# First block's down product with activations stationary, and the mixer's x kept by tokens

## The chip, the cores and the metric

One core of a Trainium2 chip runs the program. The metric is the time of one execution on the device in microseconds. Of the kernel before there are three timed runs, 919.45, 919.45 and 920.10, median 919.45, and one profiled execution. PE is the matrix engine (TensorE), DVE the vector engine (VectorE), ACT the scalar engine (ScalarE), POOL and SP the engines GpSimd and SyncE, which here mostly issue transfers (DMA). SBUF is the memory on the chip that the engines read, PSUM the eight accumulation banks that PE writes, each 128 partitions by 512 numbers here.

## The reference

One layer, 512 tokens, width 1024, all in 32-bit numbers:

```python
x = x + 0.5 * swiglu(rmsnorm(x, g1), w_gate1, w_up1, w_down1)   # first block, inner width 2816
x = x + token_mixer(rmsnorm(x, gm), w_in, w_out, ...)           # 4 differential + 8 dilated heads
x = x + 0.5 * swiglu(rmsnorm(x, g2), w_gate2, w_up2, w_down2)   # second block
return rmsnorm(x, g_final)

def swiglu(x, w_gate, w_up, w_down):
    return (jax.nn.silu(x @ w_gate) * (x @ w_up)) @ w_down

def rmsnorm(x, g):
    return x * lax.rsqrt(jnp.mean(x * x, axis=-1, keepdims=True) + 1e-6) * g
```

The mixer projects the normed x to q, k and v, takes scores with a bias by distance, exponentials, weighted values, a norm per differential head, and the product with w_out. lambda, a number from four small vectors, weighs the second map of the differential heads.

## The kernel before

**Numbers in two parts.** Each operand of a product is split into a high part (a cast to PE's rounded 32-bit type, on ACT) and a low part (the difference, on DVE). A product is three matmuls, high x high, high x low, low x high (`mm3`, L143 to L146). So every weight that arrives needs a cast on ACT and a subtraction on DVE before PE can use it. "High" and "low" below mean these two.

**Layout.** x lies by features in the first block (`x[k]`: 128 features by 512 tokens), as do its normed parts `xh[k]`, `xl[k]`.

**The two blocks (`ffn`, L225 to L1131).** A first part makes some pairs of inner columns plainly. The rest goes through `pipeline` (L835): a list of units, each with seven products of 2 x 2 blocks instead of eight (`SEVEN`, L46): a11, s3, s2, a12, s1, a22, s4, where s1 = a21 + a22, s2 = s1 + a11, s3 = a11 + a21 and s4 = s2 + a12 or alike. "g" and "u" units make pairs of gate and up columns. Their 4 x 3 matmuls per product take a weight block as the stationary operand and 256 tokens of x as the moving one.

The down product is where the two blocks differ. In the first block, six inner tiles go plainly ("p" units, weights stationary, 512 tokens moving, 18 matmuls for each of eight output tiles), and two groups of eight inner tiles go through "d" units: weights stationary, 256 columns of activation moving, four units in each group, each updating two output tiles of x (`down_step`, L815). In the second block the down product is turned: "P" units and "t" units take the activations as stationary and 512 columns of weight as moving operand (`tiles_product`, `block_product`, L583 to L658), so that their output, and x, lie by tokens. A "t" unit runs each of the seven products over four or five pairs, one pair a step, six matmuls of 512 columns a step.

**Sums of weight blocks.** s1 and s3 are made by transfers: SP loads one block of 256 KB into a slot, and POOL then issues a second transfer that adds the other block onto it (`weight_sums`, L364, for pair units; `block_load`, L471, for "t" units). s2 and s4 are made by DVE (`total`, L396).

**Order.** `pipeline` gives every piece of work a time in nominal nanoseconds, with `STEP` = 1410 as one product of one pair, and a rank. Pieces are issued by time, then by rank. A product stands at its own start; its high part 4 steps before (rank 3), its low part 3 steps before (rank 2.5), a total 5 steps before (rank 2), loads 7 to 14 steps before (`block_events`, L885, for "t" units). Within an engine the issued order is the order of execution; between engines, semaphores hold an instruction until its data is there and its buffer is free. In the mixer the lists `at` and `put` (L1301) do the same by the number of the chunk. At the end of the first block the order of DVE and ACT is left to a scheduler for the lines between the two (L1268 to L1282, lambda).

**Slots.** 44 slots of 128 x 512 numbers (`slot`, L99) serve one use after another. `PAIR_SLOTS` (L49) gives the seven tiles of a pair's activations their slots, the first of each seven holding the block b11, which a11 alone reads. Weight tiles from DRAM go through three buffers "raw", their two parts through `w_all`.

**Between block and mixer.** As the last "d" units finish an output tile, `to_mixer` (L1256) multiplies x with the mixer's gain, splits it into xh and xl, and adds its squares to `sq`. The mixer's norm is not applied to x: `rstd` (L195) makes it by eight 1-column matmuls (`st_n`) and spreads it by two more (`bc_n`), and q and k are multiplied with it when they leave PSUM (`scaled`, L1424), v when it is copied. q and k of a head pair take 8 chunks (`qk_chunks`, L1399), and attention 0 starts its scores four chunks after q0 and k0 are done (L1714). While the mixer runs, x is turned by DVE in 32 x 32 blocks, written to DRAM and read back by tokens (`turn_x`, `rows_back`, L1721 to L1732).

**Between mixer and second block.** `wo_tail` (L1888) adds the output product to x by tokens and norms each token tile: sum (DVE), squares with their total (ACT), mean (DVE), root (ACT), reciprocal (DVE), scaling (ACT). PE then turns the scaled tile to features by transposes (`turn`, L955).

Of the kernel before, what the change touches and what calls it, by code (L numbers as in the profile page):

```python
# [42 lines left out]
PAIRED = (6, 2)  # L43
PLAIN = 6
# [9 lines left out]
TURNED_PLAIN = 4  # L54
TURNED_PAIRS = ((4, 6, 8, 10), (12, 14, 16, 18, 20))
TURNED_SETS = {4: (28, 29, 30, 31, 32, 33, 34), 6: (35, 36, 37, 38, 39, 40, 41), 8: (42, 43, 12, 13, 14, 15, 4),
# [3 lines left out]
TURNED_FIRST = (26, 27)  # L60
TURNED_S3 = ((20, 21, 26, 27), (20, 21, 26, 27, "xh0"))
TURNED_S1 = ((8, 9, 11, 10), (10, 11, 9, 8, "xh2"))
TURNED_A22 = (("sq", "bc", "ob", 8), ("xh3", "xl3", "xh5", "xl5", "xh7"))
TURNED_AHEAD = {"s3": ((36, 32, 28, 24), (80, 77, 74, 71, 11)),
                "s1": ((19, 16, 13, 10), (19, 17, 15, 12, 9)),
                "a11": ((11, 10, 9, 8), (11, 10, 9, 8, 4))}
# [5 lines left out]
STEP, PLAIN_STEP, TILES_STEP = 1410, 4080, 5440  # L72
# [12 lines left out]
def tile_macaron(ctx: ExitStack, tc, xs, xT, wf, wgu1, wst1, wd1, wdg1, wqk, wvw, wv, wo, wgu2, wst2,  # L85
# [11 lines left out]
    dp = ctx.enter_context(tc.tile_pool(name="dp", bufs=1, space=DRAM))  # L97

# [126 lines left out]
    def ffn(wgu, wst, wd, wdg, n0, n1, norm, early, res, nm, hooks, ended, first=None,  # L225
            bias=None, final=None, lead=None):
# [98 lines left out]
        plain = 5  # L325
        if final is None:
            units = [("g", n1)] + pairs(n1 + 2, PLAIN + 8)
            units += [("p", m) for m in range(plain)] + [("d", 0, m) for m in range(0, KD, 2)]
            units += pairs(PLAIN + 8, JF)
            units += [("p", m) for m in range(plain, KD)] + [("d", 1, m) for m in range(0, KD, 2)]  # L330
        else:
            units = [("g", n1)] + pairs(n1 + 2, TURNED_PAIRS[0][-1] + 2) + [("P", 0), ("t", 0)]
            units += pairs(TURNED_PAIRS[1][0], JF) + [("P", 1), ("t", 1)]
        ops, begin, starts = [], {}, [0]
        for u in units:
            begin[u] = len(ops)
            for o in ((u[0],),) if u[0] in "pP" else SEVEN:
                for p in range({"t": len(TURNED_PAIRS[u[1] % 2]), "P": 2}.get(u[0], 1)):
                    ops.append((u, o, p))
                    starts.append(starts[-1] + {"p": PLAIN_STEP, "P": TILES_STEP}.get(u[0], STEP))  # L340

        def rows(u):

            if u[0] == "d":
                return wdg[u[1], u[2]], wdg[u[1], u[2] + 1]
            return [wst[u[1] + i - n1][int(u[0] == "u")] for i in range(2)]

        def sum_slots(u):
            if u[0] == "d":
                return GROUP_SUMS[u[2] // 2 % 2]  # L350
            if final is not None:
                if u == units[0]:
                    return TURNED_FIRST
                return GROUP_SUMS[(u[0] == "u") ^ (u[1] in TURNED_PAIRS[1])]
            if u == units[0]:
                return PAIR_SLOTS[0][:2]
            if u[1] == PLAIN + 8:
                return GROUP_SUMS[u[0] == "u"]
# [16 lines left out]
        def load(u, which=(0, 1)):  # L375
            raws.setdefault(u, [])
            whole = [wd[u[1]]] if u[0] == "p" else [rows(u)[0], rows(u)[1][:, 512:]]
# [5 lines left out]
        def source(t):  # L383
# [6 lines left out]
            if o[0] == "p":  # L390
                return r0[:, :PLAIN * P]
# [20 lines left out]
        def high(t):  # L412
            u, o, p = ops[t]
            if o[0] == "p":
                half.clear()
                h, l = w_place()
                made[t] = h[:, :PLAIN * P], l[:, :PLAIN * P]
            elif o[0] == "P":
# [4 lines left out]
            elif (u, o[0]) == (("t", 1), "s4"):  # L423
                made[t] = kept_weights(p)
            else:
# [10 lines left out]
                if not half:  # L436
                    h, l = w_place(odd)
                    half.extend([(h[:, :512], l[:, :512]), (h[:, 512:], l[:, 512:])])
                    if skip or t and ops[t - 1][1][0] == "p":

                        half.pop(0)
# [24 lines left out]
        def block_rows(u, p):  # L466
            r = wdg[TURNED_PAIRS[u[1]][p] // 2]
# [3 lines left out]
        def block_load(u, o, p):  # L471
# [7 lines left out]
            elif o == "a12":  # L479
                dst = parts["B", u, p] = place(TURNED_S3[u[1]][p], f"rb{nm}{u[1]}{p}")  # L480
                nc.sync.dma_start(dst, r["a12"])
            elif o == "a22":
                dst = parts["E", u, p] = place(TURNED_A22[u[1]][p], f"re{nm}{u[1]}{p}")
                nc.sync.dma_start(dst, r["a22"])
            else:
                k, tags, a, b = (("B", TURNED_S3, "a11", "a21") if o == "s3"
                                 else ("C", TURNED_S1, "a21", "a22"))
# [15 lines left out]
        def moving(u, block):  # L503

            if u[0] == "d":
                return [hs[PLAIN + 8 * u[1] + 2 * p][block] for p in range(4)]
# [33 lines left out]
        def product(t):  # L540
# [8 lines left out]
            if o[0] == "p":  # L549
                m = u[1]  # L550
                po = mm_bank(f"pd{nm}{m}")
                for k in range(PLAIN):
                    c = slice(k * P, (k + 1) * P)
                    mm3(po[:], h[:, c], l[:, c], ah[k][:], al[k][:], k == 0, k == PLAIN - 1)
                put(starts[t + 1], stt, x[m], po[:], 0.5, x[m], ALU.add)
                return
# [78 lines left out]
        def block_step(t, u, o, pw, pz, pv):  # L635
# [21 lines left out]
            if u[1] == 1:  # L657
                final(o, t, put, pz)  # L658
# [1416 lines left out]
```

## Time and profile before

| what | us |
|---|---|
| median of three runs (919.45 to 920.10) | 919.45 |
| the profiled execution, its own time | 920.74 |
| its span, from first to last instruction | 919.0 |
| PE busy in the span | 910.7 |
| DVE busy | 731.8 |
| ACT busy | 549.6 |
| POOL busy | 118.2 |

The first block's pair units run from about 84 to 294 us in the trace, its "p" and "d" units from 154 to 214 and from 290 to 346, the mixer from 346 to about 580, the second block from there to the end. How to read the rows: a row of a group gives the source line, the engine, the operation, output and inputs by the program's names, shape, count, and after the bars the busy time, the mean duration of one in ns, and the idle time of the engine ahead of it with what ended it. A matmul's row lasts longer than the spacing to the next one, since matmuls overlap in the array: 0.39 us for 512 columns, while the next may start 0.23 us later. What PE spends is therefore read from start to start. A timeline row gives start, duration, engine, line and operation.

### The profile page before, as it was taken

The page shows a single profiled execution, that of the slowest core. Times are in us where ns is not written, and L with a number is a line of the kernel's source. Part 1 is how long each engine was busy: PE and PEld are TensorE (multiplying, and loading weights), DVE is VectorE, ACT ScalarE, POOL GpSimd, SP SyncE. Part 2 cuts the span into 40 slices and gives each one's busy share as a digit, 9 for nine tenths or more (in the row PEclk, how much of TensorE's full clock was granted, in tenths as well). Part 3 has the DMA queues.
Part 4 walks back from the last instruction along what each step waited for, and adds up shares of the span by engine and source line. Part 5 has one row for each costly group of instructions (what it writes and reads, how often), then busy time and mean ns, then how long its engine had stood idle before and what let it go on. Part 6 is the DMA issues. An engine that isn't in the chain of part 4 may idle for free.

```text
span 919.0 us, 16498 instructions
## 1 busy us (share of the span) xinstructions
PE 910.7 (99%) x6014; PEld 830.8 (90%) x6014; DVE 731.8 (80%) x1525; ACT 549.6 (60%) x1155; POOL 118.2 (13%) x157
## 2 busy tenths in 40 slices
PE   9999999999999999999999999999999999999997
PEld 7888999899999998888989778989999889999885
DVE  7797888676888897968876545897887878888786
ACT  6455665345665665655776675656666446666564
POOL 0001100112111010063000000011121012211100
PEclk9999999999999999999999999999999999999999
DMA  7446645578856563457433204365798269877722
GB/s 256 125 142 159 163 120 162 154 173 206 218 139 178 147 169 109 144 154 236 132 115 116 69 24 138 92 158 168 179 232 216 82 181 242 210 180 204 199 70 92
DMA packets 64593, 143.66 MB, mean 156 GB/s; under 512 B 7872, under 2 KB 8384, under 8 KB 64512
## 3 DMA queue, kind: packets, MB, share of 16 engines
q1 hardware_dynamic: 47856, 110.93, 37.1%
q0 software_dynamic: 16656, 31.68, 20.2%
q8 instruction: 47, 0.77, 0.3%
q14 instruction: 34, 0.28, 0.1%
HBM read 135.20 MB, written 4.24 MB: 152 GB/s over the span
## 4 chain that ended last, share of the span: by engine, by line
PE 94%; DVE 3%; DMA 1%; ACT 1%; issue 1%; DVEq 0%; SPq 0%; ACTq 0%
PE pt L146 3%; PE pt L145 3%; PE pt L144 3%; PE pwo L144 2%; PE pwo L145 2%; PE pwo L146 2%; PE pua L144 2%; PE pua L145 2%; PE pua L146 2%; PE pq L144 2%; PE pq L146 1%; PE pq L145 1%; PE pk L144 1%; PE pk L146 1%; PE pk L145 1%; PE pda L146 1%
## 5 line engine op out<-in xcount | busy, mean ns | idle before, releaser
L1520 ACT ACTIVATE pr<-pr,mx 128x128 f32<-128x128 f32 (+3 forms) x64 | 36.0, 563 | 37.7 <-DVE mx L1517 37.6
L1517 DVE CUSTOM_DVE_ANT_0 pr<-sc,strip 128x128 f32<-128x128 f32 (+3 forms) x64 | 30.6, 487 | 19.6 <-PE sc L1515 19.4
L372 POOL DMA_DIRECT2D s1bg<-wst_dram x10 | 8.7, 866 | 272.9 <-DVE fin L1908 160.8
L443 ACT CAST w<-s2a 128x512 fp32r<-128x512 f32 x46 | 28.6, 621 | 16.1 <-DVE s2a L406 13.2
L447 DVE TENSOR_TENSOR w<-s2a,w 128x512 fp32r<-128x512 f32 x46 | 31.5, 686 | 6.6 <-ACT w L443 6.6
L447 DVE TENSOR_TENSOR w<-s2b,w 128x512 fp32r<-128x512 f32 x38 | 26.1, 686 | 6.8 <-ACT w L443 6.8
L1726 POOL DMA_DIRECT2D xn_rows<-xt x32 | 20.6, 654 | 64.1 <-DVE xt L1723 64.1
L443 ACT CAST w<-s2b 128x512 fp32r<-128x512 f32 x38 | 23.5, 620 | 5.7 <-DVE s2b L406 5.4
L144 PE MATMUL pq<-xh,w 128*128 128x512 f32 x64 | 26.7, 417 | 0.0
L144 PE MATMUL pwo<-w,mh 128*128 128x512 f32 x64 | 25.9, 404 | 0.0
L146 PE MATMUL pq<-xh,w 128*128 128x512 f32 x64 | 25.1, 392 | 0.0
L145 PE MATMUL pq<-xl,w 128*128 128x512 f32 x64 | 25.1, 392 | 0.0
L144 PE MATMUL pk<-xh,w 128*128 128x512 f32 x64 | 25.1, 391 | 0.0
L146 PE MATMUL pk<-xh,w 128*128 128x512 f32 x64 | 25.0, 391 | 0.0
L145 PE MATMUL pwo<-w,mh 128*128 128x512 f32 x64 | 25.0, 391 | 0.0
L146 PE MATMUL pwo<-w,ml 128*128 128x512 f32 x64 | 25.0, 391 | 0.0
L145 PE MATMUL pk<-xl,w 128*128 128x512 f32 x64 | 24.9, 390 | 0.0
L1324 DVE TENSOR_TENSOR w<-raw_qk,w 128x512 fp32r<-128x512 f32 x28 | 19.0, 687 | 4.6 <-ACT w L1320 4.5
L146 PE MATMUL pwgb<-xh,w 128*128 128x256 f32 x80 | 22.6, 282 | 0.0
L145 PE MATMUL pxgb<-ttb,w 128*128 128x256 f32 x80 | 22.5, 281 | 0.0
L145 PE MATMUL pwgb<-xl,w 128*128 128x256 f32 x80 | 22.5, 281 | 0.0
L144 PE MATMUL pwgb<-xh,w 128*128 128x256 f32 x80 | 22.5, 281 | 0.0
(712 smaller groups left out, 3945.7 us busy)
## 6 DMA issues: line engine op xcount, KB each, us to landing
raw_qk<-wqk_dram SPq DMA_DIRECT2D x16, 512.0 KB, 3.4
raw0bg<-wst_dram SPq DMA_DIRECT2D x10, 512.0 KB, 5.3
raw0bu<-wst_dram SPq DMA_DIRECT2D x9, 512.0 KB, 5.4
raw_gua<-wgu_dram SPq DMA_DIRECT2D x8, 512.0 KB, 3.3
raw0ag<-wst_dram SPq DMA_DIRECT2D x8, 512.0 KB, 4.8
raw0ad<-wdg_dram SPq DMA_DIRECT2D x8, 512.0 KB, 3.8
strip<-bias_rows SPq DMA_DIRECT2D x16, 256.0 KB, 3.8
raw_wo<-wo_dram SPq DMA_DIRECT2D x8, 512.0 KB, 3.4
```

Of the source, the lines that this page charges most:

```text
L144: T.matmul(po, wh, mh, start=first, stop=False, skip_group_check=on)
L145: T.matmul(po, wh, ml, start=False, stop=False, skip_group_check=on)
L146: T.matmul(po, wl, mh, start=False, stop=last, skip_group_check=on)
L372: nc.gpsimd.dma_start(t[:], b, accum_op=ALU.add)
L443: A.copy(made[t][0], source(t))
L447: V.tensor_tensor(l, source(t), h.bitcast(F32), op=ALU.subtract)
L1324: V.tensor_tensor(l[:, c:c + 512], raw[:, c:c + 512], h[:, c:c + 512].bitcast(F32), op=ALU.subtract)
L1517: V.tensor_tensor_reduce(out=pi, in0=ps[:, :w], in1=st["b"][m][:, w - 1::-1], op0=ALU.add, op1=ALU.min, scale=1.0, scalar=3.0e38, accum_ou ...
L1520: A.activation(pi, pi, AF.Exp, scale=-1.0, bias=st["mx"][:, m, i:i + 1], accum_out=st["ls"][:, m, i:i + 1])
L1726: nc.gpsimd.dma_start(bass.AP(tensor=ap.tensor, offset=ap.offset + m * P + a * NB, ap=[[D, NB], [NB * D, S // NB], [1, NB]]), t[a * NB:(a ...
```

## The change

1. The first block's down product is turned as in the second block. A table `TURNED` holds what differs between the blocks "a" and "b". Group 0 of block "a" is pairs 6, 8, 10, 12, group 1 pairs 14, 16, 18, 20. "p" and "d" units and `down_step` go; ("P", 0) makes the left half of the output columns for the six plain tiles, three steps of 24 matmuls. The right half's plain product is left to the seam.
2. x comes in a second time, by tokens (`xn`), loaded over x[0] to x[7] while the pair units run.
3. A new part between block and mixer, the seam: for each of four token tiles, `plain_mm` (18 matmuls of 512 columns), an addition to x, squares, mean, root, scaling, and eight transposes by PE, whose results ACT and DVE split into xh and xl with the mixer's gain. q, k and v need no scaling by the norm any more; the spread, `turn_x` and `rows_back` go.
4. The chunks of q0, k0, q1, k1 are computed for 256 tokens at a time (`early_chunk`), between the transposes; their weights are prepared in the seam. Attention 0 starts eight chunks, no longer four, after chunk 8.
5. From the pipeline of the first block to the end, PE, DVE and ACT keep the order of the program; the lines of lambda stand in it between pipeline and seam.

```diff
+EARLY_SLOTS = (((16, 17), (18, 19)), ((20, 21), (6, 7)))
...
+TURNED = {
+    "a": {"plain": PLAIN, "pairs": ((6, 8, 10, 12), (14, 16, 18, 20)),
+          "sets": {j: PAIR_SLOTS[(j - PLAIN) // 2 % 4] for j in range(PLAIN, JF, 2)},
+          "s3": ((8, 9, 10, 11),) * 2, "s1": (tuple(t[0] for t in PAIR_SLOTS),) * 2,
+          "a22": (("sq", "bc", "ob", "ob"),) * 2,
+          "ahead": {"s3": ((36, 32, 28, 24),) * 2, "s1": ((-1.6, -2.6, -3.6, -4.6),) * 2,
+                    "a11": ((11, 10, 9, 8),) * 2}},
+    "b": {"plain": 4, "pairs": ((4, 6, 8, 10), (12, 14, 16, 18, 20)),
...
+          "ahead": {"s3": ((36, 32, 28, 24), (80, 77, 74, 71, 11)),
+                    "s1": ((19, 16, 13, 10), (19, 17, 15, 12, 9)),
+                    "a11": ((11, 10, 9, 8), (11, 10, 9, 8, 4))}}}
...
-            units += [("p", m) for m in range(plain)] + [("d", 0, m) for m in range(0, KD, 2)]
...
-            units += [("p", m) for m in range(plain, KD)] + [("d", 1, m) for m in range(0, KD, 2)]
...
+        units = [("g", n1)] + pairs(n1 + 2, groups[0][-1] + 2) + [("P", 0), ("t", 0)]
+        units += pairs(groups[1][0], JF) + [("P", 1)] * (close is None) + [("t", 1)]
...
+            if close is not None:
+                for i in range(KD):
+                    at((10 + 5 * i) * STEP, 2.9, nc.sync.dma_start, x[i],
+                       xn[i % 4 * P:(i % 4 + 1) * P, i // 4 * S:(i // 4 + 1) * S])
+                close(at, starts[begin["t", 1]], starts[-1], ah, al)
...
-            if o[0] in TURNED_AHEAD:
-                at(starts[begin[u]] - TURNED_AHEAD[o[0]][u[1]][p] * STEP, 2.2, block_load, u, o[0], p)
+            if o[0] in shape["ahead"]:
+                at(starts[begin[u]] - shape["ahead"][o[0]][u[1]][p] * STEP, 2.2, block_load, u, o[0], p)
             elif o[0] in ("a12", "a22"):
                 at(now - 8 * STEP, 1.5, block_load, u, o[0], p)
...
             if o[0] in ("s2", "s4"):
                 at(now - 5 * STEP, 2, total, t)
             at(now - 4 * STEP, 3, high, t)
             at(now - 3 * STEP, 2.5, low, t)
...
+        order.close()
+        ordered.enter_context(tc.manual_schedule(engines={mybir.EngineType.PE, mybir.EngineType.DVE,
+                                                          mybir.EngineType.Activation}))
+        with tc.manual_schedule(engines={mybir.EngineType.SP, mybir.EngineType.Pool}):
             pipeline()
...
+    def close(at, begin, end, ah, al):
+        closing["tiles"] = ah, al
+        for time, rank, f, *a in ((begin + 3 * STEP, 1.5, plain_load, 0),
+                                  (begin + 9 * STEP, 4.5, plain_high, 0),
+                                  (begin + 10 * STEP, 2.5, plain_low, 0),
+                                  (begin + 22.3 * STEP, 1.5, plain_load, 1),
+                                  (begin + 24.3 * STEP, 1.5, plain_load, 2),
+                                  (begin + 24.4 * STEP, 1.6, early_load, 0, 0),
+                                  (begin + 18.5 * STEP, 5, A.activation, root[:], eps[:], AF.Sqrt),
+                                  (end - 2.8 * STEP, 3.5, plain_high, 1),
+                                  (end - 1.8 * STEP, 2.6, plain_low, 1),
+                                  (end - 1.7 * STEP, 1.6, early_load, 0, 1),
+                                  (end - 0.9 * STEP, 3.5, plain_high, 2),
+                                  (end, -1, plain_low, 2)):
+            at(time, rank, f, *a)
...
+        def chain(tt):
+            t = now[0]
+            ev(t + 0.1, add, tt)
+            ev(t + 0.8, squared, 1, tt)
+            ev(t + 1.6, mean, tt)
+            ev(t + 2.0, root_part, tt)
+            for dh in range(2):
+                ev(t + 2.7, scaled, dh, tt)
...
+        ev(-1, V.tensor_scalar_mul, sm[:, KD:2 * KD], sm[:, KD:2 * KD], 2.0)
+        for t, tt in ((0.2, 0), (0.9, 1), (2.9, 2), (3.6, 3)):
+            ev(t, squared, 0, tt)
+        for t, u, hf, c, n in ((1.6, 0, 0, 0, 1024), (6.4, 0, 1, 0, 1024), (10.4, 1, 0, 0, 512),
+                               (11.0, 1, 0, 512, 512), (18.8, 1, 1, 0, 512), (19.5, 1, 1, 512, 512)):
+            ev(t, early_high, u, hf, c, n)
+            ev(t + 1.1, early_low, u, hf, c, n)
...
+        for tt in range(NQ):
+            pe(4.09, plain_mm, tt)
+            chain(tt)
+            if tt in (1, 2):
+                pe(0.8, turn, tt - 1)
+            if tt == 2:
+                split(0, now[0])
+        for c in range(16):
+            if c in (1, 4):
+                pe(0.8, turn, 2 + c // 4)
+            if c == 4:
+                split(1, now[0])
+            pe(1.36, step, c)
+        for _, _, f, a in sorted(todo, key=lambda e: (e[0], e[1])):
+            f(*a)
...
-            attention(int(w[1]), len(chunks) + (4 if w[1] == "0" else 3 if w[1] == "7" else 5))
+            attention(int(w[1]), len(chunks) + (8 if w[1] == "0" else 3 if w[1] == "7" else 5))
```

The small routines of the seam: `plain_high` and `plain_low` split the right half of the six plain tiles' weights, `early_high` and `early_low` those of q0, k0, q1, k1; `gathered` splits a transposed tile; `split` issues it for all eight tiles of a side; `squared` leaves the sum of a row's squares beside it; `add` is the half of the product added onto x.

456 lines of the change are left out of this document (221 added, 235 removed), and 10 rows, old and new, of tables (TURNED, TURNED_SETS).

## The prediction

> **What bounds the kernel now.** I read the page's busy times first, then the table of who waited for whom on PE, then a table of windows over the stages that the change touches.
>
> ```profile
> span 919.0 us, 16498 instructions
> PE 910.7 (99%) x6014; PEld 830.8 (90%) x6014; DVE 731.8 (80%) x1525; ACT 549.6 (60%) x1155; POOL 118.2 (13%) x157
> ```
> ```profile
> engine line waited for: us in total, times, longest us
> PE warm L1143 <- POOL ones_d L1137: 1.0, 1, 1.0
> PE sc L1515 <- DMA l<-l: 0.4, 1, 0.4
> PE pga L1188 <- ACT w L1168: 0.3, 1, 0.3
> ```
>
> PE never waits after the start: 1.7 us in all, 0.4 of it in the mixer. So an edit on another engine can gain next to nothing, an edit of PE's stream counts fully, and every new wait of PE lengthens the kernel by its own length. The profiled execution took 920.74 us, 1.7 more than its span and 1.3 more than the median of the three runs, 919.45; I put the sum of differences on the median.
>
> **PE's stream.** Columns of the windows: window, length, busy time (instructions) of PE, weight loads, DVE, ACT, POOL; clock; DMA share; GB/s. They are the two "d" groups, the start of the mixer, and the first turned group of the second block.
>
> ```profile
> 174.30:214.00 39.70, 39.70 (x337) 39.67 (x336) 31.63 (x60) 20.46 (x41) 6.95 (x8) 1.00 0.69 180
> 305.90:346.20 40.30, 40.22 (x338) 40.01 (x337) 37.57 (x75) 30.79 (x68) 4.66 (x6) 1.00 0.65 169
> 716.40:754.50 38.10, 38.10 (x170) 31.55 (x169) 28.82 (x48) 17.53 (x31) 3.48 (x4) 1.00 0.46 134
> ```
> ```profile
> 585.91 0.60 PE L960 MATMUL xt<-ident,y 128*128 128x128 f32 x4
> 586.26 0.36 PE L144 MATMUL pgb<-xh,guhb 128*128 128x256 f32 x1
> 586.46 0.28 PE L145 MATMUL pgb<-xl,guhb 128*128 128x256 f32 x1
> 586.58 0.28 PE L146 MATMUL pgb<-xh,gulb 128*128 128x256 f32 x1
> 350.15 0.92 PE L200 MATMUL st_n<-ones_d,sq 128*128 128x1 f32 x7
> ```
>
> - A "d" group is 4 units x 7 products x 12 = 336 matmuls of 256 columns. Less one and two of neighbours, the windows hold 39.6 and 40.1 us, 0.119 us each. A "t" group of four pairs is 168 matmuls of 512 columns; less two, 38.0 us, 0.226 each, so one step of six takes 1.36 us. Two groups: 76.0 for 79.7, **-3.7 us**.
> - The plain part stays 144 matmuls of 512 columns (72 in ("P", 0), 72 in the seam): 0.
> - q0/k0 and q1/k1 go by halves of the tokens: 192 matmuls of 256 columns (22.9 us) for 96 of 512 (21.8): **+1.1**.
> - 32 new transposes: four take 0.35 us from start to start, and the next matmul's spacing is 0.20 for 0.12: 8 x 0.44 = **+3.5**.
> - The mixer's means go (eight 1-column matmuls, 0.9) and its spread (two of 512, 0.45): **-1.3**.
>
> The stream comes to -0.4 us. The clock is 1.00 in all windows, so nothing is to be had there. What else goes is off PE and worth 0 while PE waits for none of it: the 16 products of q and k with the spread, the eight VectorE turns of x and the 40 POOL transfers through DRAM. The eight loads of xn (rows of x) go on SP between the pair units, 5 steps apart; they would cost only if a weight load behind them came late, and those are issued 7 steps ahead.
>
> **The turned groups in the first block.** In block_events the block sums C = a21 + a22 ("s1") are loaded at -1.6, -2.6, -3.6, -4.6 steps *ahead*, that is after the group's start, for their slots 6, 28, 34, 41 hold the b11 blocks that the four a11 steps read. (The second block loads them 10 to 19 steps before.) The first load thus waits on SP for PE's first step, 1.36 us. It is two legs: SP writes a21, POOL adds a22.
>
> ```profile
> s1ad<-wdg_dram SPq DMA_DIRECT2D x8, 256.0 KB, 3.8
> s3ad<-wdg_dram SPq DMA_DIRECT2D x8, 256.0 KB, 4.3
> s1ad<-wdg_dram POOLq DMA_DIRECT2D x8, 256.0 KB, 4.4
> s3ad<-wdg_dram POOLq DMA_DIRECT2D x8, 256.0 KB, 5.6
> sCb<-wdg_dram SPq DMA_DIRECT2D x9, 256.0 KB, 5.4
> sCb<-wdg_dram POOLq DMA_DIRECT2D x9, 256.0 KB, 5.5
> ```
> ```profile
> DMA to landing us min/median/max: 2.5/3.7/9.4
> ```
> ```profile
> DMA to landing us min/median/max: 3.6/5.2/8.4
> ```
> ```profile
> 338.46 0.69 DVE L408 TENSOR_TENSOR s2a<-raw0ad,s2a 128x512 f32<-128x512 f32 x1
> 339.06 0.69 DVE L447 TENSOR_TENSOR w<-s1ad,w 128x512 fp32r<-128x512 f32 x1
> ```
>
> (KB each and median us from issue to landing; then the spread for the SP legs of the pair units' sums, and for their POOL legs; then two neighbouring VectorE operations: 0.60 us apart, 0.69 until the result.) By the s1ad legs the first C lands at 1.4 + 3.8 + 4.4 = 9.6 us after the group's start. The three behind it follow 1.36 us apart if each leg takes as long, 2.1 if they crowd as s3ad does behind s1ad (issued 0.4 later: 0.4 + 4.3 + 5.6 against 8.2).
>
> What waits: total("s2", 0), which adds C to A, stands on VectorE at begin + 3 steps, *ahead* of the low half of s3's third block (same time, rank 2 before 2.5); the totals of p = 1, 2, 3 stand ahead of the low halves for s3's fourth, s2's first and s2's second. VectorE takes its queue in order, so PE waits for low halves whose own data have long landed. The walk, in us from the group's start, C at 9.6, 11.0, 12.3, 13.7: total 9.6, low 10.2 to 10.9, so s3's third step starts at 10.9 and not 6 x 1.36 = 8.2; the next low ends at 12.3, s3's fourth step starts there; then 13.7 and 15.0 for s2's first and second, which stood at 12.2. Stall 2.8. With 2.1 between the landings the same walk gives 17.2, stall 5.0. I take the middle, **3.9 us a group, 7.8 in two**. Ends: with the fastest legs (2.5 + 3.6, 1.36 apart) C lands from 7.5 on, the walk ends at 12.9, 0.7 a group; with the sCb legs (10.9, 2.1 apart) 7.7. I stay by the s1ad rows, the nearest: the same weight tensor and block. Later steps have leads of several steps again; what was lost stays lost, for PE has no slack.
>
> [...]
>
> **The seam.** After the last group, PE goes on with plain_mm, four token tiles of 18 matmuls (4.1 us each), turn(0) behind the second, turn(1) behind the third, then sixteen early chunks. Time 0 is the end of the last turned step. Now that VectorE and ScalarE keep program order here, the lambda lines (L1270 to L1282 of before) stand between the last two updates of x and the seam, not scattered among other work as before:
>
> ```profile
> 343.14 0.28 DVE L1270 TENSOR_TENSOR lp<-lt 128x128 f32<-128x128 f32 x1
> 344.27 0.28 DVE L1272 TENSOR_REDUCE ls<-lp 128x2 f32<-128x128 f32 x1
> 347.10 0.16 DVE L1282 TENSOR_TENSOR nlam<-nlam,keep 128x1 f32<-128x1 f32 x1
> 343.87 1.28 ACT L1273 ACT_TABLE_LOAD   x1
> 345.17 0.20 ACT L1273 ACTIVATE ls<-ls 128x2 f32<-128x2 f32 x1
> L135 ACT CAST w<-raw_gua 128x1024 fp32r<-128x1024 f32 x8 | 8.4, 1048 | 11.5 <-PE pua L145 11.5
> L136 DVE TENSOR_TENSOR w<-raw_gua,w 128x1024 fp32r<-128x1024 f32 x8 | 9.8, 1221 | 1.9 <-ACT w L135 1.9
> 566.83 0.69 DVE L1895 TENSOR_TENSOR x<-pwo,x 128x512 f32<-128x512 f32 x1 [0.40 <-PE pwo L146]
> 567.55 0.63 ACT L1898 ACTIVATE junk_n<-x 128x512 f32<-128x512 f32 x1 [2.23 <-DVE x L1895]
> 568.50 0.20 ACT L1905 ACTIVATE fin<-fin 128x1 f32<-128x1 f32 x1 [0.23 <-DVE fin L1903]
> 569.38 1.34 ACT L1915 ACTIVATE y<-x,fin 128x512 f32<-128x512 f32 x2 [0.68 <-DVE fin L1911]
> ```
>
> VectorE: two updates to 1.3, lp, sum, the exponential on ScalarE (its table load lies before), five small ones 0.2 apart: free at about 3.2. ScalarE squares x tiles 0 and 1 to 3.5 and casts wqh0 to 4.6; VectorE's rest of it runs to 5.8 and two more sums to 6.1. Only then comes add(0), though plain_mm(0) ended at 4.1. Its square ends at 7.6; the exponential has thrown out the square-root table loaded before, so a load of 1.28 stands ahead of the root: 9.1. Behind the root ScalarE first casts wqh1 (1.05), then scales y: 10.2 to 10.9. turn(0) could have started at 8.2: **+2.7 us**. After it there is room: turn(1), due at 15.7, has y at about 14.8; turn(2) and turn(3) have chunks ahead of them. Ends: 0, if add(0) starts at 4.3 and needs the 3.3 us that the rows show from add to a scaled tile; 4.4, if one more cast of 1.05 and a second scaling of 0.67 fall ahead of the first transpose. I take the walk. The other weight casts and the two more table loads (back to exp) lie beside PE.
>
> [...]
>
> Attention 0 now meets attention 1 in mixer steps 21 to 25. By the 0.60 spacing VectorE falls about 1 us behind at most, and a score bank is needed a step (1.36 us) later: 0, at most +1.
>
> **Sum.** -0.4 + 7.8 + 2.7 = +10.1: 919.45 + 10.1 = **929.5 us**.
>
> **Rivals.**
> - *The sums come in time.* If C lands before 8.2 - 1.3 = 6.9 us after the group's start, no low half is late: the groups cost 0, the seam 2.7, total 921.7. For it: DMA is busy only 0.46 of a turned group. Against: 1.4 plus the two fastest legs, 6.1, is 7.5. [...] Chance 0.08.
> - *The leads cover all (the other side).* Casts stand 3 to 4 steps ahead of their products, and in the run before this lead hid every such wait. Should the lead hold at both places, the stream alone decides: 919.0, no change. It decides from: C landed by 6.9, y scaled by 8.2. Against: the totals stand in the queue. Chance 0.08.
> - *The sums crowd.* sCb's legs in both groups: 15.4 + 2.7 - 0.4, total 937.2. For it: the rows of the second block, with the same four-fold pattern. Against: pair units' sums were being loaded there. Chance 0.12.
> - *The change gains.* It would need two microseconds off PE's stream, which only counting matmuls at a faster pace could give. Chance 0.06.
>
> **How the numbers follow.** The forecast has 0.66. A measurement tells 0.2%, 1.8 us, from no change. Slower is the forecast, the crowded sums and half of the first rival: 0.82; within: the other half and the covered leads: 0.12; faster 0.06. The range, 920.5 to 936, leaves out the gain, the covered leads and the upper part of the crowded case, 0.2 in all. The forecast's own range is 924 to 934.
>
> **What would show it.** In the profile after, PE's waits should name low halves (w on VectorE) in two places with 3 to 5 us each, VectorE's idle time ahead of total should name the DMA of sCa, and the seam should show some 2.7 us before the first transposes, with three table loads near it. A matmul of a turned group should be 0.226 us apart outside the waits. Wrong I am if C lands by 7 us, if the low halves are done before the totals, or if PE waits somewhere I hold for covered: SP's order between the strips, raw_c2 and the q weights, or the P tiles.

## The result, and the profile after

The changed kernel takes 945.32 us (median of four runs, 944.20 to 946.97) beside 919.78 for the kernel before in the same session: ratio 1.0276, 95% interval 1.0257 to 1.0295. Forecast were 929.5 us and a range of 920.5 to 936. The direction was right; the forecast loss of 10.1 us was less than half of the 25.5 that came. The profiled execution took 946.97 us, 1.65 above the median.

The page's busy times, then the table of who waited for whom on PE in the changed kernel:

```profile
span 945.2 us, 15975 instructions
PE 920.9 (97%) x5796; PEld 828.0 (88%) x5796; DVE 713.1 (75%) x1480; ACT 554.0 (59%) x1162; POOL 93.4 (10%) x117
```
```profile
engine line waited for: us in total, times, longest us
PE pt L154 <- DVE w L440: 10.6, 2, 5.5
PE xt L1332 <- ACT y L1322: 3.3, 1, 3.3
PE po L1707 <- DVE q L1538: 1.5, 1, 1.5
PE warm L1103 <- POOL ones_d L1097: 1.0, 1, 1.0
PE pga L1148 <- ACT w L1128: 0.5, 1, 0.5
PE sc L1632 <- DVE mx L1635: 0.5, 1, 0.5
```

PE had 1.7 us of waits before and has 17.6 now. The two largest stand where the prediction put them: a low half on VectorE in each turned group of the first block, and the first transposes of the seam. But these 15.9 us more of waiting are not the 26.2 us by which the two profiled spans differ. The table of windows over the two groups and the seam (up to the first product of q0) shows most of what is missing, in the clock's column (0.93, 0.93, 0.86; the columns are those of the prediction's windows):

```profile
171.62:217.62 46.00, 40.94 (x169) 33.30 (x168) 30.33 (x49) 18.73 (x32) 6.91 (x8) 0.93 0.65 166
297.14:343.77 46.63, 41.10 (x171) 33.30 (x169) 33.54 (x57) 25.06 (x50) 4.61 (x6) 0.93 0.60 163
343.77:368.18 24.41, 21.12 (x89) 17.35 (x88) 14.38 (x41) 14.82 (x33) 0.00 (x0) 0.86 0.34 105
```

A group was to take 38.0 plus 3.9; it takes 46.0 and 46.6. The chain of work that ended last tells how in group 0 (start, duration, what):

```profile
172.92 0.24 PE pt L155
173.18 2.56 DMA sCa<-wdg_dram
175.76 0.04 POOLq L483
175.81 0.47 issue
176.29 7.50 DMA sCa<-wdg_dram
...
183.88 0.06 DVE raa L399
...
184.49 0.69 DVE w L440
...
185.23 0.79 PE pt L154
186.02 0.43 PE pt L155
...
190.72 0.27 PE pt L154
190.99 0.23 PE pt L155
```

PE's first step frees the slot, SP writes a21 (2.56 us), POOL adds a22 (7.50, issued half a microsecond after a21 has landed), VectorE adds the sum to a11 (L399), makes the low half that stands behind it (L440), and PE goes on at 185.23. That is link by link the walk of the prediction. The first C lands 12.2 us after the group's start (171.62), not 9.6; by the trace the four land at 12.2, 14.2, 15.5 and 17.4 us, in group 1 at 12.8, 14.8, 16.3 and 18.7. Behind the wait PE's matmuls are 0.43 us apart until 190.7, and 0.23 from there: half speed.

In the seam, the same table in steps of 2 us, from the wait on:

```profile
351.00:353.00 2.00, 1.09 (x5) 0.56 (x3) 0.50 (x2) 1.55 (x3) 0.00 (x0) 1.00 0.78 233
353.00:355.00 2.00, 0.00 (x0) 0.00 (x0) 1.19 (x5) 1.99 (x4) 0.00 (x0) 0.88 0.07 29
355.00:357.00 2.00, 1.62 (x9) 1.66 (x9) 1.57 (x2) 0.56 (x2) 0.00 (x0) 0.50 0.02 6
...
359.00:361.00 2.00, 2.00 (x7) 1.52 (x6) 1.27 (x2) 0.73 (x2) 0.00 (x0) 0.50 0.01 4
361.00:363.00 2.00, 2.00 (x10) 1.62 (x9) 0.00 (x0) 0.00 (x0) 0.00 (x0) 0.91 0.78 211
```

While PE stands still the granted clock falls to 0.50, and it stays there for some 6 us after the work has begun again.

### The profile page after: what moved, and what is told of

Read it like the earlier page. It is cut to its first block, busy times and chain, and to the rows that moved or that the text cites. A ratio compares the mean times of both kernels' runs of the same rounds, so it can differ in the third digit from the quotient of the medians.

```text
span 945.2 us, 15975 instructions
## 1 busy us (share of the span) xinstructions
PE 920.9 (97%) x5796; PEld 828.0 (88%) x5796; DVE 713.1 (75%) x1480; ACT 554.0 (59%) x1162; POOL 93.4 (10%) x117
## 4 chain that ended last, share of the span: by engine, by line
PE 90%; DVE 3%; DMA 3%; ACT 2%; issue 1%; DVEq 0%; SPq 0%; POOLq 0%; ACTq 0%
PE pt L154 5%; PE pt L155 5%; PE pt L153 5%; DMA sCa<-wdg_dram 2%; PE pq L153 2%; PE pq L155 2%; PE pk L155 2%; PE pk L153 2%; PE pq L154 2%; PE pk L154 2%; PE pwo L153 2%; PE pua L155 1%; PE pua L153 1%; PE pua L154 1%; PE pwo L155 1%; PE pwo L154 1%
## 5 line engine op out<-in xcount | busy, mean ns | idle before, releaser
L528 DVE SCALAR_TENSOR_TENSOR x<-pt,x 128x512 f32<-128x512 f32 x46 | 30.0, 686 | 11.8 <-PE pt L155 11.8
L436 ACT CAST w<-raa 128x512 fp32r<-128x512 f32 x24 | 14.8, 621 | 31.6 <-DVE raa L399 20.8
L440 DVE TENSOR_TENSOR w<-s2b,w 128x512 fp32r<-128x512 f32 x38 | 26.0, 685 | 6.8 <-ACT w L436 6.8
L440 DVE TENSOR_TENSOR w<-s2a,w 128x512 fp32r<-128x512 f32 x30 | 20.6, 686 | 6.8 <-ACT w L436 6.8
L154 PE MATMUL pt<-w,h3a 128*128 128x512 f32 x32 | 14.7, 459 | 10.6 <-DVE w L440 10.6
L436 ACT CAST w<-s2a 128x512 fp32r<-128x512 f32 x30 | 18.6, 620 | 6.7 <-DVE s2a L404 5.7
L1435 DVE TENSOR_TENSOR w<-raw_qk,w 128x512 fp32r<-128x512 f32 x24 | 16.4, 687 | 7.9 <-ACT w L1431 7.8
L1538 DVE SCALAR_TENSOR_TENSOR q<-pq,q 64x512 fp32r<-64x512 f32 x16 | 11.0, 689 | 14.6 <-ACT q L1535 14.4
L1632 PE MATMUL sc<-k,q 128*128 128x128 f32 (+3 forms) x64 | 20.7, 325 | 0.5 <-DVE mx L1635 0.5
L1633 PE MATMUL sc<-l,q 128*128 128x128 f32 (+3 forms) x64 | 20.3, 322 | 0.0
L154 PE MATMUL pxub<-ttb,w 128*128 128x256 f32 x72 | 20.2, 281 | 0.0
```

The source lines that it names most:

```text
L154: T.matmul(po, wh, ml, start=False, stop=False, skip_group_check=on)
L436: A.copy(made[t][0], source(t))
L440: V.tensor_tensor(l, source(t), h.bitcast(F32), op=ALU.subtract)
L528: V.scalar_tensor_tensor(o, a, f, b, op0=ALU.mult, op1=op1)
L1435: V.tensor_tensor(l[:, c:c + 512], raw[:, c:c + 512], h[:, c:c + 512].bitcast(F32), op=ALU.subtract)
L1538: V.scalar_tensor_tensor(o, a, -(HD ** -0.5), h.bitcast(F32), op0=ALU.mult, op1=ALU.subtract)
```

## The experiments

My theory: three things lose the time. The block sums C come late in both groups; the lines of lambda hold up the seam; a wait costs more than its length, since the clock falls. Its rivals are named in each expectation. Where a run is compared with the changed kernel, 945.3 is meant; times of groups and seam come from windows like those above.

### s2 from s3 and a22

```diff
 def total(t):
+    if nm == "a" and o[0] == "s2":
+        V.tensor_tensor(ta, parts["B", u, p], parts["E", u, p], op=ALU.add); return
-    "a22": (("sq", "bc", "ob", "ob"),) * 2,
+    "a22": (("bc", "ob", "ob", "sq"),) * 2,
     "ahead": {...
+              "a22": ((0.9, 0.6, 0.3, 0.1),) * 2,
```

> In block a, total makes s2 as s3 + a22 (the same sum) in place of C + a11. Both operands are plain transfers or landed long before: s3 is loaded 24 to 36 steps ahead, a22 is loaded 0.1 to 0.9 steps ahead of the group into places that are free there. C = a21 + a22 is still loaded as before, but is then needed only by the s1 steps, 16 steps after the group's start. Theory (the block sums C land too late, 12.3 and 12.8 us after the group's start, and nothing else holds the groups): PE waits for no low half in either group, each takes 38.1 to 38.5 us in place of 46.0 and 46.6, and the clock stays at 1.00 there; 945.3 - 16 = 929 us. Rival (the transfers crowd: the sixteen legs of a group are just too much for the stretch): the wait moves to the lows of a12 or s1, whose loads now also wait for the totals; the groups then still lose 3 us or more each, 935 us or above.

927.46 us, ratio to the kernel before 1.0076 [1.0059, 1.0093]. The windows of the two groups:

```profile
169.53:207.62 38.09, 38.09 (x169) 31.53 (x168) 30.27 (x49) 18.32 (x32) 6.96 (x8) 1.00 0.72 173
287.14:325.27 38.13, 38.13 (x171) 31.53 (x169) 33.42 (x57) 24.72 (x50) 4.62 (x6) 1.00 0.70 179
```

PE is busy throughout and the clock is at 1.00. The adding transfers still run, and C lands as late as ever (in group 0 at 12.5 to 18.4 us after the start); it only isn't needed then. So 7.9 and 8.5 us, 16.4 in all, were the price of waiting for C in s2, and nothing else holds the groups.

### Totals later in VectorE's queue

```diff
+    if nm == "a" and o[0] == "s2":
+        at(now - 3.9 * STEP, 2, total, t); at(now - 3.85 * STEP, 3, high, t)
+        at(now - 3 * STEP, 2.5, low, t); return
```

> Order alone: in block a the total of s2 is issued 1.1 steps later and the high half behind it, so that on VectorE the totals stand behind all four low halves of s3. Nothing else differs. Theory (VectorE's queue turns the late sum into an early wait): PE runs through all four s3 steps and stops only at s2's first step, 10.9 us after the start, until total, cast and low half are done, about 12.3 + 2.0 = 14.3: 3.4 us of wait per group in place of 5.2 and 5.7, and the rest as before if the clock still falls: 942 us; 939 if the clock stays at 1.00. Rival (the place in the queue does not matter, only the landing): 945 us, same waits as before.

945.60 us, ratio 1.0271 [1.0253, 1.0290]: nothing gained. PE's waits in the stretch of group 0:

```profile
PE pt L153 <- ACT w L436: 3.4, 2, 2.9
PE pt L154 <- DVE w L440: 1.1, 2, 0.8
```

In group 0 PE does run through s3, and then stops four times at high and low halves of s2. In group 1 it stopped at s3 all the same, 3.9 us, for another low half of VectorE (h4a) that now stood behind the totals. The groups took 46.75 and 46.89 us.

But something else moved with the order. SP's rows for the last a12 loads of group 0, first in the changed kernel, then in this run:

```profile
177.69 9.86 SPq L474 DMA_DIRECT2D rba<-wdg_dram  x3
```
```profile
175.45 2.01 SPq L474 DMA_DIRECT2D rba<-wdg_dram  x3
```

With the low halves of s3 made early, their slots come free early. SP issues the last two loads of a12 at 6.5 and 7.5 us after the group's start (13.6 and 15.6 in the changed kernel) and the first three of a22 from 8.1 to 9.4 (16.0 to 16.9), into the stretch in which C is on its way, and the last C lands at 19.9 us for 17.4. So the run shows that this order gains nothing as a whole. What the place in VectorE's queue costs while C lands as before it doesn't show.

### PE kept busy during its waits

```diff
+    if nm == "a" and o[0] == "s3" and p == 2:      # 22 matmuls into a bank nobody reads
+        for i in range(22): T.matmul(idle[:], ..., start=True, stop=True)
+    for i in range(14 * (tt == 0)):                # and 14 ahead of the first turn
+        T.matmul(ts[side][3][:], ..., start=True, stop=True)
```

> Adds matmuls whose result nobody reads, at the three places where PE waits longest: 22 of 512 columns ahead of s3's third step in each group of block a (5.0 us), 14 ahead of the first turn in the seam (3.2 us). Theory (a wait of PE costs twice: its own length, and then a stretch at half clock, 2.65, 2.76 and 2.9 us by the matmuls that take 0.427 for 0.227): the added matmuls fill the waits, the clock stays at 1.00 after them, the seam saves 2.9, and each group saves 1.3 (the sums behind the first land 1.3 to 2.0 us apart, which the half clock covered before): 939 to 940 us although PE has 13.2 us more to do. Rival (the slow matmuls have another cause, for instance the operands' arrival): the added matmuls change nothing, 945 us, or cost their overhang over the waits.

943.34 us, ratio 1.0251 [1.0235, 1.0266]. The windows of group 0, group 1 and seam:

```profile
170.21:216.90 46.69, 44.28 (x192) 35.36 (x190) 30.36 (x49) 18.57 (x32) 6.96 (x8) 1.00 0.69 163
296.42:343.39 46.97, 44.66 (x192) 35.27 (x191) 33.45 (x57) 25.09 (x50) 4.62 (x6) 1.00 0.61 162
343.39:365.04 21.65, 21.52 (x103) 17.72 (x102) 14.42 (x41) 14.87 (x33) 0.00 (x0) 1.00 0.38 118
```

58 more matmuls of 512 columns, 13 us of work, went into the idle time, and they keep the clock at 1.00. But in the groups no gain is seen (46.69 and 46.97 for 46.00 and 46.63): PE arrives sooner at sums that land 1.3 to 2.0 us one behind the other, and most of the half speed lay under the wait for the next sums. There my theory of a double price is not borne out. A gain of half a microsecond would not be seen here: the first C landed at 13.4 and 13.3 us after the start, 1.2 and 0.5 later than in the changed kernel. In the seam nothing is late afterwards, and it takes 21.65 for 24.41.

How much the clock costs behind a wait of 3.3 us isn't fixed. The undisturbed seam is 18.14 (below). With that wait, untouched, it took 24.41 here, 22.94 in the run with s2 from s3, and 21.64 in the run with later totals, where the clock stayed at 1.00: 6.3, 4.8 and 3.5 us more. Behind the waits of over 5 us the clock always fell to half (the groups of the changed kernel and of the next three runs below, where such waits stand, have a mean clock of 0.89 to 0.93); behind one of 3.3 it fell or not (seams at 0.86, 0.93 and 1.00). In the changed kernel the three stretches at 0.50 that began in waits of PE last 6.8 us each: 183.9 to 190.7, 310.1 to 317.0 and 354.5 to 361.3, by windows of 0.25 us. Other runs had shorter and longer ones: a mean clock of 0.93 over the 22.94 us of the seam in the run with s2 from s3, and one of 0.89 over the 47.58 us of group 0 in the run with the root's table back, make estimates of some 3 and some 10 us at 0.50.

### Lambda behind the seam

```diff
-    lt = tp.tile(...); ...; A.activation(ls[:], ls[:], AF.Exp); ... nlam ...
     ffn(...); ...
     seam(step)
+    lt = tp.tile(...); ...; A.activation(ls[:], ls[:], AF.Exp); ... nlam ...
```

> The lines of lambda are moved from ahead of the seam to behind its last chunk; nothing else. Theory (they delay the first norm: ScalarE's first square waits for the exponential, the exponential throws out the table of the root, 1.28 us): squares and casts run 1.5 to 2 us earlier, no table load stands ahead of the first root, the first turn starts 1 to 1.5 us after plain_mm(1) in place of 3.45, and the clock stays at 1.00: 940 us. Rival (the weight casts ahead of add(0) set it, lambda only costs its table load): the wait is still above 2 us, 942 to 944 us. If the clock falls all the same, 943.

940.17 us, ratio 1.0216 [1.0201, 1.0231]. What had stood in the changed kernel's seam, from its timeline:

```profile
346.67 0.20 ACT L1383 ACTIVATE ls<-ls 128x2 f32<-128x2 f32 x1 [1.71 <-DVE ls L1382]
346.78 0.62 ACT L1314 ACTIVATE sq<-x 128x512 f32<-128x512 f32 x1
...
350.66 0.68 DVE L1311 SCALAR_TENSOR_TENSOR x<-pc,x 128x512 f32<-128x512 f32 x1
352.17 1.28 ACT L1280 ACT_TABLE_LOAD   x1
```

and the seam of the run without lambda:

```profile
342.86 0.63 ACT L1314 ACTIVATE sq<-x 128x512 f32<-128x512 f32 x1
347.34 0.69 DVE L1311 SCALAR_TENSOR_TENSOR x<-pc,x 128x512 f32<-128x512 f32 x1 [0.48 <-PE pc L155]
343.06:361.20 18.14, 18.14 (x89) 15.17 (x88) 12.94 (x34) 12.07 (x30) 0.00 (x0) 1.00 0.47 143
```

The first square starts before the group has ended (342.86 for 343.06), add(0) (the rows of L1311) waits for PE's product, where in the changed kernel PE's first transpose came to wait for what follows from add(0), and the seam takes 18.14 with no wait at all. The time fell by 5.1 us, less than the 6.3 of the seam: in this profile group 1 took 47.71 for 46.63, and the first scores waited 0.8 for 0.5. I had expected 1 to 1.5 us to stay; the squares ran further ahead than I thought.

### The root's table loaded back at once

```diff
     A.activation(ls[:], ls[:], AF.Exp)
+    A.activation(root[:], eps[:], AF.Sqrt)
```

> The changed kernel with one more root on ScalarE straight behind lambda's exponential, so that its table is loaded again there and not between the first mean and its root. Theory (lambda costs the seam two things: ScalarE and VectorE start on the squares and casts some 2 us late, and 1.28 us of table load stand ahead of the first root): only the second moves, and it still stands in ScalarE's queue ahead of the squares, so the chain to the first turn hardly shortens: seam 23 to 24.5 us, 944 to 945. Rival (the table load alone is the matter): the wait falls from 3.45 to 2.2, the clock stays at 1.00, seam 20.2, 941 us.

946.25 us, ratio 1.0279 [1.0261, 1.0298]; wait 3.7, seam 24.62. The load of 1.28 us left the place ahead of the root and delayed the first square by 1.5 us. Lambda costs the seam its place in ScalarE's queue, with the table load as one part of that.

### C's competitors behind it

```diff
-    nc.sync.dma_start(dst, r["a12"])                # and a22 alike
+    (nc.gpsimd if nm == "a" else nc.sync).dma_start(dst, r["a12"])
```

> The changed kernel, but in block a the loads of a12 and a22 are issued by POOL, behind its adding transfers (the first a12 ahead of the fourth), in place of SP, where they stand between and behind the first legs of C. Nothing else differs. Theory (C lands at 12.3 us and not at 9.6 because the eight legs of C and the loads of a12 are in flight together, DMA share about 1.0 from 180 to 187 us): with fewer in flight the first C lands at 9.6 to 10.5 us and the last before 15, group 0 takes 42.5 to 44 us, in all 939 to 942. Rival (four adding transfers at once are as slow by themselves): first C at 12 us or later, groups 46 us, 945, or more if a12 then comes late.

944.24 us, ratio 1.0261 [1.0239, 1.0284]. In group 0 the first C landed at 181.93, 11.7 us after the start of the group (170.27), the last at 16.3 (12.2 and 17.4 in the changed kernel); in group 1 they landed at 13.2 and 17.5 (12.8 and 18.7). The groups took 46.5 and 46.1. The competitors account for about 1.1 us at the last C and for nothing certain at the first; the rival holds, C's own eight legs are enough to make it late.

### Sums by VectorE, no adding transfers

```diff
 def block_load(u, o, p):
     ...
     nc.sync.dma_start(dst, r[a])
+    if nm == "a" and o == "s1":                     # a22 plainly; total adds it onto C
+        nc.sync.dma_start(e, r[b]); return
     nc.gpsimd.dma_start(dst, r[b], accum_op=ALU.add)
 ...
```

> The changed kernel, but in block a C = a21 + a22 is made by VectorE from two plain transfers of SP; the a22 that comes for it stays for the a22 steps, so that a group moves four legs fewer and none that adds. The loads start as late as in the changed kernel (1.6 us after the group's start, for the same slots), and the totals stand at the same place in VectorE's queue, 0.6 us longer each. Theory (the late landing is a matter of transfer time: by the page, POOL's queue takes 17.9% of 16 engines' 945.2 us for 27.48 MB, 1.6 us for 256 KB, SP's 37.4% for 113.02 MB, 0.82 us; eight plain legs, four adding ones and the first a12 make 13 us of all engines, and C's landings, 12.2 to 17.4 us after the start, follow it): eleven or twelve plain legs are 9 to 10 us, the first C is there at 5 to 6.5 us, the groups take 38.1 to 39.5 us, 929 to 931. Rival (the late start of the first leg sets it): first C at 9 us or later, groups 41 us and more, 935 or above.

934.96 us, ratio 1.0160 [1.0147, 1.0174]. First the transfers of the changed kernel between 171 and 192 us (queue: packets, MB, share of 16 engines; then transfers, KB, median us to landing):

```profile
q1 hardware_dynamic: 1566, 2.86, 42.2%
q0 software_dynamic: 576, 1.05, 31.3%
sCa<-wdg_dram SPq DMA_DIRECT2D x4, 256.0 KB, 3.9
sCa<-wdg_dram POOLq DMA_DIRECT2D x4, 256.0 KB, 6.8
rba<-wdg_dram SPq DMA_DIRECT2D x4, 256.0 KB, 4.4
```

then this run's windows of the two groups:

```profile
169.61:210.07 40.46, 39.30 (x169) 31.22 (x168) 32.92 (x53) 18.54 (x32) 3.49 (x4) 1.00 0.58 162
289.59:333.50 43.91, 39.93 (x170) 31.15 (x169) 36.09 (x61) 25.02 (x50) 1.06 (x2) 1.00 0.49 149
```

Of 21 us, POOL's queue took 0.313 x 21 = 6.6 us of all 16 engines for four adding transfers, 1.64 each; SP's took 0.422 x 21 = 8.9 for 2.86 MB, 0.81 for 256 KB. An adding transfer uses the engines twice as long as a plain one. That is the adding and not the queue: in the run before, from 170.27 to 191 us, POOL's queue also carried seven plain transfers of 256 KB.

```profile
q0 software_dynamic: 1118, 2.84, 57.5%
```

Of 20.73 us these are 11.9; four adding ones (1.05 MB) at 1.64 leave 5.4 for the 1.79 MB of the plain ones, 0.79 for 256 KB.

Four plain legs, four adding ones and four of a12 make 13 us; from the first issue (173.18) to the last C it took 15.9. Without the adding ones both parts of the first C were there 5.1 us after the start and the last at 11.4 (7.6 and 13.5 in group 1), from the same late first issue. So C was late through its transfers, not through the late start. Three things went at once here, the adding, POOL's queue and the order of the two legs, for a22 no longer waits until a21 has landed; what each did to the landing was not told apart. In the changed kernel the first C spent 3.1 us on a21 and the handover to POOL, and 7.5 on the adding leg. The groups stay above 38.1, as PE still waits for low halves, 1.1 us in group 0 and 3.9 in group 1: VectorE has an addition more, and the last parts land late; 930 us was too hopeful.

### Both cures, and the rest of the gap

```diff
 # s2 from s3 and a22, and lambda behind the seam; no other edit
```

> Both cures at once: s2 made as s3 + a22 in block a, and the lines of lambda behind the seam. Theory (two separate places, each loses on its own): groups 38.1 and 38.1 us (46.0 and 46.6 in the changed kernel), seam 18.1 (24.4): 945.3 - 7.9 - 8.5 - 6.3 = 922.6 us, and what is left over the kernel before, 2.5 us, lies in the mixer: a wait of the last values product for a bank (1.5) and two of the first attentions (about 1). Rival (the seam's room comes from the stalls ahead of it: once the second group runs through, weights or x are late in the seam): the seam stays at 19.5 us or above, 924 us or more.

922.90 us, ratio 1.0035 [1.0022, 1.0048]: groups 38.09 and 38.12, seam 18.14. The two places add up.

```diff
 def evac_now(first):
     if first:
         tiles()
+        for n, b0, ps in (("tq", 28, st["pq"]), ("tk", 30, st["pk"])):
+            st[n] = slot(b0, f"{n}{u}"); V.tensor_copy(st[n][:], ps[:])
-    pq, pk = st["pq"], st["pk"]
+    pq, pk = st["tq"], st["tk"]
```

> As the run with both cures, and for the two head pairs that are split at once (0 and 7) VectorE first copies q and k from PSUM to SBUF, as the products with the spread did in the kernel before; the splits then read the copies. Theory (the products with the spread were not only scaling, they freed the PSUM bank: without them the bank of q7 is held until its last low half, and the values product of attention 7 waits 1.5 us for it): that wait goes, 921.2 us. Rival (the two copies of 0.69 us delay the splits, and the scores behind them wait instead): no change, or up to 1.4 us more.

921.76 us, ratio 1.0018 [1.0008, 1.0027]; the wait of 1.5 us is gone. (The time fell by 1.1 us, and the two intervals overlap; the row tells it more surely.) In the changed kernel's timeline the values product starts when the last low half has read q7's bank (first two rows); the kernel before had emptied the bank by a product with the spread 4 us ahead (last row):

```profile
553.19 0.69 DVE L1538 SCALAR_TENSOR_TENSOR q<-pq,q 64x512 fp32r<-64x512 f32 x1 [2.18 <-ACT q L1535]
554.03 2.37 PE L1707 MATMUL po<-ptx,v 128*64 128x512 f32 x16 [1.52 <-DVE q L1538]
```
```profile
524.17 0.69 DVE L1427 SCALAR_TENSOR_TENSOR tq<-pq,rbc_n 128x512 f32<-128x512 f32 x1 [2.42 <-PE pq L146]
```

```diff
-    attention(int(w[1]), len(chunks) + (8 if w[1] == "0" else 3 if w[1] == "7" else 5))
+    attention(int(w[1]), len(chunks) + (6 if w[1] == "0" else 3 if w[1] == "7" else 5))
```

> As the run with both cures and the copies, and attention 0 starts its scores at chunk 14 in place of 16, so that it meets attention 1 in two chunks fewer. Theory (the waits of 0.8 and 0.5 us at the first scores and the first turned maps come from the two attentions meeting on VectorE and ScalarE): they go or halve, 920.6 to 921.2 us, even with the kernel before (920.2). Rival (scores two chunks earlier meet the splits of q1 and of the transposed x instead): 921.8 or above.

923.16 us, ratio 1.0040 [1.0025, 1.0054]: the rival, 1.4 us worse than without. The first scores then wait 0.8 us for the low halves of k, which stand just ahead of them, and 0.5 for a bank.

```diff
-    seam(step); lambda's lines
+    put(9, 9, lam_lines); seam(step)
```

> As the run with both cures and the copies, but the lines of lambda stand in chunk 9 of the mixer, behind the split of the last transposed tiles, and no longer behind chunk 15, where their table load (1.28 us) and eight short operations stand on ScalarE and VectorE just ahead of the first scores. Theory (they are what makes the scores of attention 0 wait 0.8 us at their third pair): that wait goes or halves, 921.0 us. Rival (the wait comes from the two attentions and the splits of q1 alone): 921.8, same wait.

920.15 us, ratio 1.0006 [0.9997, 1.0015]. No wait at the scores is left, of 0.8 us in the run with the copies; the fall of the time by 1.6 us is at the edge of what the two intervals can tell.

```diff
-    ... + (8 if w[1] == "0" else 3 if w[1] == "7" else 5)
+    ... + (8 if w[1] == "0" else 7 if w[1] == "1" else 3 if w[1] == "7" else 5)
```

> As the run with lambda in chunk 9, and attention 1 starts two chunks later (at chunk 23 in place of 21), so that it meets attention 0 in two chunks less. If the two attentions meeting cost the rest (0.5 us at the first turned maps): 920.5 us, even with the kernel before (920.2). If it only moves what attention 1 needs into its later work: same as the run with lambda in chunk 9 or up to 1 us more.

919.58 us, ratio 0.9999 [0.9990, 1.0008], even with the kernel before. PE waits 1.3 us in all, at the program's start; the groups take 38.09 and 38.12, the seam 18.14. It differs from the run before it by less than the two intervals can tell. None of the versions beats the kernel before.

## Why the prediction was wrong

| term | predicted | measured | shown by |
|---|---|---|---|
| PE's stream | -0.4 | -0.3 (919.58 beside 919.87, interval ±0.8) | the last run, where PE waits for nothing |
| two turned groups | +7.8 | +16.4 | 46.00 and 46.63 to 38.09 and 38.13 |
| the seam | +2.7 | +6.3: wait 3.3, clock 2.9 | 24.41 to 18.14 |
| q and k no longer through a copy | 0 | +1.5 | the wait for the bank of q7, gone with the copies |
| first scores | 0 to +1 | +0.5 | its wait in the table of the changed kernel; gone in the run with lambda in chunk 9 |

The measured column adds up to 24.4 of the 25.5 us; the 1.1 that is left was not traced.

**The stream** was right as far as the runs can tell: the turned groups take 76.2 us where nothing holds them (forecast 76.0), and there was nothing to win. **The groups**: place, links and VectorE's queue were as described; with C at 12.2 the prediction's own walk gives a first wait of 12.2 + 1.3 - 8.2 = 5.3, and the profile shows 5.06 and 5.53. With all four landings the same walk gives stalls of 6.5 and 7.7 us, of the 7.9 and 8.5 lost. So the walk was sound and what went into it was not. The step that failed is "By the s1ad legs the first C lands at 1.4 + 3.8 + 4.4 = 9.6 us": I added the median landing times of transfers elsewhere. The plain leg took 2.6 us, less than the 3.8 assumed, but the adding leg 7.5 and not 4.4, and 0.5 between the two was left out. C's own eight legs, four of them adding, stand in one stretch and share the same 16 engines, of which the two queues took 42.2% and 31.3% between 171 and 192 us. The busy share of 0.46 that I gave for the rival is a mean over 38 us of a group of the second block, where these loads start long before; here, from 179 to 187 us, it stood at 0.8 to 1.1.

"The sums crowd" was named as a rival, at 7.7 a group and a chance of 0.12, and was the nearest to the truth: its rows, sCb's, put the first C at 1.4 + 5.4 + 5.5 = 12.3 (the 10.9 of the prediction is the legs alone). That it hit so closely is in part luck: those sums stood two to three steps apart, among those of the pair units, and their legs were alike, where the measured ones are 2.6 and 7.5. "The sums come in time" asked for the first C before 6.9 us, so for two legs in 5.5; it landed at 12.2, and the adding leg alone took 4.5 to 7.6 us in the four sums of group 0 (median 6.8).

How much the place in VectorE's queue added to it stays open: in the run with the totals later C itself landed later.

**The seam**: lambda in program order on the path, as written, wait 3.3 for 2.7. What failed is "The clock is 1.00 in all windows, so nothing is to be had there": nothing to win, but something to lose, and no price for it stood at any of the three waits. In the seam it was nearly as much as the wait, in this profile; in the groups no run shows it, and the stalls of the walk leave at most 1.4 and 0.8 us for it.

**The mixer**: "What else goes is off PE and worth 0 while PE waits for none of it" failed for the products with the spread, for its condition did not hold. They were off PE, but they emptied a PSUM bank, and PE waited 1.5 us for that bank. That the attentions meet cost nothing that a run could show once lambda stood in chunk 9. The 0.5 us at the scores in the changed kernel went in the runs with both the copies and lambda elsewhere; which of the two took it was not told apart.

The start of the program (up to the first plain product) took 153.0 to 155.3 us in these profiles, 155.29 in that of the changed kernel and 153.91 in that of the kernel before. These 1.4 us of its profile are no effect of the change: the other runs with the same start have less.

## What to carry to other kernels

Cost a burst of transfers by engine time, not by the landing time of one: bytes times the queue's share per byte, summed over all that is in flight, set against the stretch in which they are needed; adding transfers count double here (1.64 us of the 16 engines beside 0.81 for 256 KB). When an instruction goes away, ask what else it did besides its arithmetic: emptying a bank (1.5 us of PE's waiting here), and standing at a certain place in a queue. On an engine that never waits, a new wait can have a second price, a clock that falls: in the seam, behind a wait of 3.3 us, it was 0.2 to 3.0 us more. In the groups, where the next sums were late behind the wait, filling the waits kept the clock at 1.00 and gained nothing (46.69 and 46.97 us for 46.00 and 46.63).

## What the runs showed of the hardware

- An adding transfer of 256 KB by POOL's queue took 1.64 us of all 16 DMA engines, a plain one by SP's 0.81, and a plain one by POOL's 0.79.
- In the changed kernel each of the three stretches at half clock that began in a wait of PE (one in each group, one in the seam) lasted 6.8 us. After a wait of PE the granted clock stood at 0.50 for some 6 us of renewed work in the changed kernel (185.2 to 190.7, and the seam from 355 to 361). A wait of 3.3 us cost the seam between 0.2 and 3.0 us beyond its length.
- 58 matmuls that nobody reads, put where PE would have stood idle, kept the clock at 1.00 and cost 0.3 to 0.7 us a group at most.
